# Holding an adaLN result back until the blocks of h are out, in a one-core decoder trunk

## The chip, the cores and the metric

One core of one Trainium2 chip runs the whole program in one launch. The metric is the device time of an execution in microseconds (us), here the median of several. A profile is one execution recorded by the hardware. PE is TensorE (PEld its weight loads), ACT is ScalarE, DVE is VectorE, POOL is GpSimd and SP is SyncE, which here issues the loads of the weights.

## The reference, cut to what matters

There are two layers of three sub-layers each, so six in a row, for 288 tokens (256 of a prompt, 32 of eight short sequences). Each sub-layer normalizes x, scales and shifts it (adaLN), runs its own mixing, normalizes the result, gates it and adds it to x.

```
def _pre(x, c, g_pre, ada_w, ada_b):
    mod = jax.nn.silu(c) @ ada_w + ada_b
    shift, scale, gate = jnp.split(mod[:, None, :], 3, axis=-1)
    return _rms_norm(x, g_pre) * (1 + scale) + shift, gate

def _post(x, y, gate, g_post, res_w):
    return x + res_w * (1 + gate) * _rms_norm(y, g_post)
```

Sub-layers 0, 2, 3 and 5 are SwiGLU feed-forwards, sub-layer 1 is windowed attention beside a gated linear recurrence (the even mixer), and sub-layer 4 is HGRN2 (the odd mixer). The adaLN product `silu(c) @ ada_w` depends on c alone, so it can be worked out at any time before its sub-layer needs it.

## The kernel before

Activations lie with features on the 128 partitions, in eight blocks of 128 features by 288 tokens. Every fp32 product is made of three: weights and activations are split into a high and a low part (`whi`, `wlo` from `raw`; `h` in two halves), and PE adds high by high, high by low and low by high in one PSUM tile. `pj` is an input projection, `y` an output projection.

The order of PE's and SP's instructions is that in which the program writes them. The other engines' instructions are put in order by the framework's scheduler, except where the program ties them into chains. To choose the order of PE's work the program keeps a clock of its own while it writes (`clk["t"]`), with a guess of how long each instruction takes. Where this clock says that PE would wait (`until`), the program inserts a piece of adaLN product as a filler (`ada_next`, `ada_half`) or a warming product (`warm`). Work with several stages is a generator in a list of `sides`; `run_sides` resumes each one when the program's clock has reached the time at which its inputs should be ready.

The adaLN product of a sub-layer comes in twelve chunks, eight for shift and scale and four for the gate, each a 1 MB load `aw` by SP and four matmuls `ada` (or eight on half the columns). A full set ends in `ada_finish`: ACT copies the PSUM tile `ada` to `asb`, PE transposes and folds it (`adaT`), and DVE makes `mod` and `modA` or `modG` from it.

Between two sub-layers (a crossing; there are five) everything depends on the tokens' sums. `out_proj` works out the two inverse roots, PE spreads them over the partitions (`yivb`, `xivb`), and `pre` makes the eight blocks of h: DVE updates x and makes `hv`, POOL scales the samples' part, ACT writes the high part of `h`, DVE the low part. ACT, DVE and POOL do this in chains `da`, `dv` and `dg`; on ACT an activation table (`tab`) follows. Then `proj_in` begins with a group of four output tiles over the eight blocks, 96 products `pj` in all, block by block as h comes. `x_stats`, a side with ACT squares (`xsq`), POOL adds and PE sums (`xms`), starts about then too. In the even mixer POOL also issues its loads and the copies of old cache rows, and it fills the edges of the convolution's input (`xr<-cin`) and takes its new state out (`rgo<-xr`).

Of the kernel before, what the change touches and what calls it, by code (L numbers as in the profile page):

```python
# [49 lines left out]
def tile_trunk(ctx: ExitStack, tc: tile.TileContext, I: dict, O: dict):  # L50
    nc = tc.nc
    SY = nc.sync
    clk = {"t": 0.0, "dma": 0.0, "step": 0.0}
# [86 lines left out]
    def flat(name, dt=F32):  # L140
        return bp.tile([128, 2 * PW], dt, tag="b", name=name)

    def dbl(name, dt=F32, w=NT):
        return flat(name, dt).rearrange("p (c t) -> p c t", c=2)[:, :, :w]

    def tmp(name, w=NT):
        return tp.tile([128, PW], F32, tag="t", name=name)[:, :w]

    def small(name, shape, tag=None, bufs=None):
        return sp.tile(shape, F32, tag=tag or "s%d" % int(np.prod(shape[1:])), name=name, bufs=bufs)  # L150

    def aux_ps(name):
        return ps.tile([128, 512], F32, tag="ps", name=name, bufs=8)
# [59 lines left out]
    def act(out, in_, f, **kw):  # L213
        r = A.activation(out, in_, f, **kw)
        if last_table[0] is not None:
            tc.add_manual_dep(r.ins, last_table[0], NOSYNC, reason="activation table order")
        last_table[0] = r.ins.name
        return r
# [32 lines left out]
    def side(gen, *aps):  # L251
        sides.append([max(clk["t"], ready(*aps)), gen])
# [180 lines left out]
    def mod_of(i):  # L433
        if i not in mods:
            mods[i] = (mp.tile([128, 24, 9], F32, tag="mod", name=f"mod{i}", bufs=3),
                       mp.tile([128, 8, 9], F32, tag="modA", name=f"modA{i}", bufs=3),
                       mp.tile([128, 8, 9], F32, tag="modG", name=f"modG{i}", bufs=3))
        return mods[i]
# [9 lines left out]

    def ada_finish(i, g, acc):
        mod, mA, mG = mod_of(i)  # L450
        asb = flat("asb")[:, :512]
        A.activation(asb, acc, AF.Copy)
        yield [asb]
        pt = aux_ps("adaT")
        o, nj = (16, 2) if g else (0, 4)
        for b in range(4):
            if g:
                T.matmul(pt[:, 18 * b:18 * b + 18], lhsT=asb[:, 128 * b:128 * b + 128], rhs=foldg, start=True, stop=True)
            else:
                T.transpose(pt[:, 128 * b:128 * (b + 1)], asb[:, 128 * b:128 * (b + 1)], ident)  # L460
        m = 9 if g else 32
        V.tensor_tensor(
            out=mod[:, o:o + 4 * nj, :].rearrange("p (j b) m -> p b j m", b=4),
            in0=pt[:, :4 * nj * m].rearrange("p (b j m) -> p b j m", b=4, j=nj)[:, :, :, 0:9],
            in1=adab[:, 24 * i + o:24 * i + o + 4 * nj].rearrange("p (j b) -> p b j", b=4).unsqueeze(3)
            .to_broadcast([128, 4, nj, 9]),
            op=OP.add)
        V.scalar_tensor_tensor(out=mG if g else mA, in0=mod[:, 8 + 8 * g:16 + 8 * g, :], scalar=1.0,
                               in1=(gph if g else gpre)[:, 8 * i:8 * i + 8].unsqueeze(2).to_broadcast([128, 8, 9]),
                               op0=OP.add, op1=OP.mult)  # L470
# [20 lines left out]
    def ada_steps(parts):  # L491
        n = ada_st["n"]
        ada_st["n"] += 1
        i, c = chunks[n]
        ada_load_to(n)
        g = int(c >= NC0)
        if c in (0, NC0):
            ada_st["acc"] = aux_ps(f"ada{i}{g}")
        acc = ada_st["acc"]
        w = aw[n][0]  # L500
        m = 512 // parts
        for q in range(parts):
            if q:
                yield
            for j in range(4):
                k = 2 * (c - NC0) + j // 2 if g else c
                T.matmul(acc[32 * j:32 * j + 32, m * q:m * q + m], lhsT=sc[:, k, :],
                         rhs=w[:, 512 * j + m * q:512 * j + m * q + m],
                         start=c in (0, NC0) and q == 0, stop=c in (NC0 - 1, NCH - 1) and q == parts - 1)
        ada_load_to(n + AW)  # L510
        if c in (NC0 - 1, NCH - 1):
            side(ada_finish(i, g, acc))
# [21 lines left out]
    def table(f):  # L534
        return act(small("tab", [128, 1]), eps, f)
# [40 lines left out]
    def spread(u, name, gap):  # L576
        until(u, gap=gap, step=ada_half)
        p = aux_ps(name)[:, :NT]
        for j in range(4):
            T.matmul(p[:, NG * j:NG * j + NG], lhsT=pick[:, j, :], rhs=u, start=True, stop=True)  # L580
        return p

    def x_stats(prior=None):
        w = small("xw", [128, NG], tag="xw", bufs=2)
        clk["xw"] = w
        if prior:
            yield 12.0
        t0 = flat("xsq")[:, :2 * NT]
        for b in range(0, NB, 2):
            t = flat("xsq")[:, :2 * NT] if b else t0  # L590
            r = A.activation(t, x[:, b:b + 2, :].rearrange("p c t -> p (c t)"), AF.Square)
            if prior:
                after(r, prior)
            if b:
                (G if prior else V).tensor_tensor(out=t0, in0=t0, in1=t, op=OP.add)
        yield
        p = aux_ps("xms")[:, :NG]
        for c in range(2):
            sums(p, t0[:, NT * c:NT * c + NT], c == 0, c == 1)
        V.tensor_scalar(out=w, in0=p, scalar1=EPS, scalar2=None, op0=OP.add)  # L600

    def h_tiles():
        hp = [mp.tile([128, 2, 2, NT], F32R, tag=f"h{u}", name=f"h{u}", bufs=1) for u in range(NB // 2)]
        for t in hp:
            parts[t.tensor.name] = {}
        return hp, [hp[b // 2][:, b % 2] for b in range(NB)]
# [3 lines left out]
    def h_mark(b, lo):  # L610
        h_times[b, lo] = clk["end"]
# [36 lines left out]
    def pre(i, iv, ivx, ys, v, a, g):  # L648
        mod, mA, _ = mods[i]
        hp, hk = h_tiles()  # L650
        vt = {}

        def view(b, n, t):
            return t[:, b:b + n, :] if n > 1 else t[:, b, :]

        def wide(p, n):
            return p.unsqueeze(1).to_broadcast([128, n, NT]) if n > 1 else p

        def update(b, n):
            y, xb = ys(b, n), view(b, n, x)  # L660
            v.tensor_tensor(out=y, in0=y, in1=wide(iv, n), op=OP.mult)
            v.tensor_tensor(out=xb, in0=xb, in1=y, op=OP.add)

        def scale(b, n):
            t = dbl(f"hv{b}") if n > 1 else tmp(f"hv{b}").unsqueeze(1)
            for q in range(n):
                vt[b + q] = (t, q)
            v.tensor_tensor(out=t if n > 1 else t[:, 0, :], in0=view(b, n, x), in1=wide(ivx, n), op=OP.mult)
            ts = t[:, :, NPR:].rearrange("p b (s t) -> p b s t", t=TS)
            for m, op in ((mA, OP.mult), (mod, OP.add)):  # L670
                g.tensor_tensor(out=ts, in0=ts, in1=m[:, b:b + n, 1:9].unsqueeze(3).to_broadcast([128, n, NSQ, TS]), op=op)
            for q in range(n):
                c = b + q
                p = t[:, q, :NPR]
                a.activation(hk[c][:, 0, :NPR], p, AF.Identity, scale=mA[:, c, 0:1], bias=mod[:, c, 0:1])
                if q == 0:
                    a.activation(hp[b // 2][:, b % 2:b % 2 + n, 0, NPR:], t[:, :, NPR:], AF.Copy)
                h_mark(c, 0)
                a.activation(p, p, AF.Identity, scale=mA[:, c, 0:1], bias=mod[:, c, 0:1])

        def low(b, n):
            h = hp[b // 2][:, b % 2:b % 2 + n]
            v.tensor_tensor(out=h[:, :, 1, :], in0=vt[b][0], in1=h[:, :, 0, :].bitcast(F32), op=OP.subtract)
            for q in range(n):
                h_mark(b + q, 1)

        update(0, 1)
        scale(0, 1)
        update(1, 1)
        scale(1, 1)  # L690
        low(0, 1)
        update(2, 2)
        scale(2, 2)
        low(1, 1)
        update(4, 2)
        scale(4, 2)
        low(2, 2)
        update(6, 2)
        scale(6, 2)
        low(4, 2)  # L700
        low(6, 2)
        return hk
# [88 lines left out]
    def out_proj(i, nk, hk):  # L791
# [105 lines left out]
        iv = spread(u, "yivb", GAPS[2])  # L897
        ivx = spread(ux, "xivb", GAPS[3])
        hk = pre(i + 1, iv, ivx, ys, dv, da, dg)
        da.add(table(AF.Sigmoid if i % 3 == 0 else AF.Silu))  # L900
        clk["prior"] = (da.last, dv.last)
        if i < NSUB - 2:
            side(x_stats(da.last))
        return hk
# [727 lines left out]
```

## Time and profile before

| what | value |
|---|---|
| median of 3 runs | 1341.95 us (1340.23 to 1341.97) |
| the profiled execution's own time | 1341.75 us |
| its span, first to last instruction | 1340.0 us |
| what lies around the span | 1.75 us |
| PE busy | 1277.4 us, 95% of the span |
| TensorE's mean granted clock | 0.981 of full |

PE is nearly always busy, so the time is close to PE's work and its gaps. The crossings' spreads `xivb` start at 262.7, 421.6, 656.9, 884.7 and 1108.5 us; the even mixer lies between the first two. PE's fp32 matmuls are recorded twice each, so `adaT x8` is four instructions.

### The profile page before, as it was taken

To read this page: it belongs to the slowest core of one execution; us is meant where nothing else is said; L and a number is where in the kernel's file an instruction comes from. 1 tells how busy PE (TensorE), PEld (TensorE's weight loads), DVE (VectorE), ACT (ScalarE), POOL (GpSimd) and SP (SyncE) were. 2 spreads that over 40 slices of the span, in tenths; PEclk is the share of its full clock that TensorE was granted. 3 is DMA by queue.
4 is the path that set the end of the run, shared out by engine and by line. 5 is a ranking of instruction groups with operands and counts; after the bars stand their busy time and mean duration, and the time that the engine had idled before them with its cause. 6 is when DMAs were issued, how large, how long until landed. Compare 5 with 4: busy or idle time off the path is not lost.

```text
span 1340.0 us, 25184 instructions
## 1 busy us (share of the span) xinstructions
PE 1277.4 (95%) x10381; PEld 1182.8 (88%) x10381; DVE 781.6 (58%) x1411; ACT 636.9 (48%) x1087; POOL 198.3 (15%) x298
## 2 busy tenths in 40 slices
PE   9999999969887999999999999999999998999996
PEld 8999999857666899999889999987878988999995
DVE  6634545538738355555655555558888877555432
ACT  5434444446645454444454444454534566444441
POOL 0000002054013100002110000225333231000011
PEclk9999999979989999999999999999999999999998
DMA  8777465477545754454566455467444352555441
GB/s 360 270 299 262 179 224 212 153 261 266 211 191 189 281 190 158 162 180 162 192 259 242 158 167 179 159 227 305 171 162 159 134 182 71 189 170 176 158 158 36
DMA packets 39555, 263.46 MB, mean 197 GB/s; under 512 B 4932, under 2 KB 5764, under 8 KB 9360
## 3 DMA queue, kind: packets, MB, share of 16 engines
q1 hardware_dynamic: 35280, 249.09, 50.9%
q0 software_dynamic: 4160, 12.77, 2.8%
q8 instruction: 81, 1.33, 0.4%
q14 instruction: 34, 0.28, 0.1%
HBM read 254.69 MB, written 7.15 MB: 195 GB/s over the span
## 4 chain that ended last, share of the span: by engine, by line
PE 83%; DVE 7%; ACT 4%; issue 2%; DMA 1%; POOL 1%; SPq 0%; DVEq 0%; POOLq 0%; ACTq 0%
PE pj L94 48%; PE y L94 24%; PE ada L94 3%; DVE wlo L94 1%; PE lv L94 1%; POOL hv L94 1%; PE adaT L94 1%; ACT hv L94 1%; DVE x L94 1%; ACT whi L94 1%; DVE hv L94 1%; ACT L94 1%; PE o L94 1%; DVE yg L94 1%; ACT h L94 1%
## 5 line engine op out<-in xcount | busy, mean ns | idle before, releaser
L94 PE MATMUL pj<-h,whi 128*128 128x288 f32 x3552 | 724.4, 299 | 2.0 <-ACT h L94 1.8
L94 PEld LDWEIGHTS pj<-h,whi 128*128 128x128 f32 x3552 | 571.0, 189 | 31.4 <-issue 19.6
L94 DVE TENSOR_TENSOR wlo<-raw,whi 128x1024 fp32r<-128x1024 f32 x326 | 399.9, 1237 | 301.6 <-ACT whi L94 301.1
L94 ACT ACTIVATE whi<-raw 128x1024 fp32r<-128x1024 f32 x326 | 340.6, 1057 | 381.8 <-PE pj L94 154.0
L94 PE MATMUL pj<-h,wlo 128*128 128x288 f32 x1776 | 519.1, 295 | 0.9 <-DVE wlo L94 0.9
L94 PEld LDWEIGHTS pj<-h,wlo 128*128 128x128 f32 x1776 | 336.1, 189 | 1.5 <-DVE wlo L94 1.4
L94 PE MATMUL y<-mh,whi 128*128 128x288 f32 x1408 | 281.3, 295 | 0.0
L94 PEld LDWEIGHTS y<-mh,whi 128*128 128x128 f32 x1408 | 226.0, 188 | 2.1 <-issue 1.7
L94 PE MATMUL y<-mh,wlo 128*128 128x288 f32 x704 | 208.0, 295 | 0.0
L94 POOL TENSOR_TENSOR yss<-yss,ysq 128x288 f32<-128x288 f32 x55 | 59.3, 1079 | 812.6 <-ACT ysq L94 804.9
L94 PEld LDWEIGHTS y<-mh,wlo 128*128 128x128 f32 x704 | 132.5, 188 | 0.0
L94 DVE TENSOR_TENSOR fs<-fs,pj 128x288 f32<-128x288 f32 x88 | 39.5, 452 | 94.8 <-PE pj L94 93.1
L94 PE MATMUL ada<-aw,cT 128*32 128x256 f32 (+1 forms) x696 | 68.9, 500 | 1.5 <-DMA aw<-in_w_ada 1.5
L94 ACT ACTIVATE mh<-fs 128x288 fp32r<-128x288 f32 x88 | 37.7, 433 | 56.1 <-DVE fs L94 56.1
L94 ACT ACTIVATE fs<-pj 128x288 f32<-128x288 f32 x88 | 34.7, 399 | 38.9 <-PE pj L94 38.9
L94 DVE TENSOR_TENSOR mh<-fs,mh 128x288 fp32r<-128x288 f32 x88 | 39.5, 452 | 10.2 <-ACT mh L94 10.2
L94 PE MATMUL y<-o,whi 128*128 128x288 f32 x192 | 39.1, 297 | 0.5 <-DVE o L94 0.5
L94 ACT ACTIVATE ysq<-y 128x288 f32<-128x288 f32 x42 | 17.0, 404 | 47.4 <-PE y L94 47.4
L94 ACT ACT_TABLE_LOAD x27 | 34.6, 1283 | 7.6 <-DVE oivw L94 5.4
L94 PEld LDWEIGHTS ada<-aw,cT 128*32 128x32 f32 x696 | 17.3, 111 | 21.6 <-issue 15.2
L94 ACT ACTIVATE h<-hv,mod,modA 128x256 fp32r<-128x256 f32 x40 | 23.7, 592 | 21.0 <-DVE hv L94 21.0
L94 DVE TENSOR_TENSOR yg<-y,modG 128x32 f32<-128x32 f32 x48 | 8.9, 186 | 40.6 <-ACT yg L94 40.6
(287 smaller groups left out, 1090.4 us busy)
## 6 DMA issues: line engine op xcount, KB each, us to landing
raw<-in_wf_in SPq DMA_DIRECT2D x88, 1024.0 KB, 4.9
aw<-in_w_ada SPq DMA_DIRECT2D x64, 1024.0 KB, 6.5
raw<-in_wf_out SPq DMA_DIRECT2D x44, 1024.0 KB, 4.9
raw<-in_wo_in SPq DMA_DIRECT2D x16, 1024.0 KB, 7.2
awf<-in_w_ada SPq DMA_DIRECT2D x8, 1024.0 KB, 9.3
raw<-in_we_in SPq DMA_DIRECT2D x7, 1024.0 KB, 7.1
raw<-in_we_out SPq DMA_DIRECT2D x4, 1024.0 KB, 8.1
S<-in_s POOLq DMA_DIRECT2D x16, 256.0 KB, 5.9
```

The source lines that it names most:

```text
L94: r = f(*args, **kw)
```

## The change

At the end of `pre` the program notes when, by its own clock, the last block of h is done (`clk["busy"]`, taken before the table is loaded) and keeps it as `clk["hold"]`. An `ada_finish` that is resumed before that time yields until it, and only then has ACT copy the result. One that is resumed before `pre` was written sees the hold of an earlier crossing, which has passed, and is not held.

```
     def ada_finish(i, g, acc):
         mod, mA, mG = mod_of(i)
+        if clk["t"] < clk.get("hold", 0.0):
+            yield clk["hold"] - clk["t"] + 0.01
         asb = flat("asb")[:, :512]
         A.activation(asb, acc, AF.Copy)
         yield [asb]
...
         hk = pre(i + 1, iv, ivx, ys, dv, da, dg)
+        clk["busy"] = clk["end"]
         da.add(table(AF.Sigmoid if i % 3 == 0 else AF.Silu))
         clk["prior"] = (da.last, dv.last)
+        clk["hold"] = clk["busy"]
```

The numbers of products `pj` and `y`, of warming products and of chunks stay as they were (some chunks are cut in halves that were whole, and the other way), but because the program's clock runs on differently, fillers and sides move in the whole program behind the first crossing. On PE at the first crossing (`adaT` folds the gate of sub-layer 1, `ada` is a chunk of a later one), this piece of the difference stands just behind the first eight `pj`:

```order
 L94 MATMUL pj_2998<-h_2894,whi 128x288
 L94 MATMUL pj_2998<-h_2894,wlo 128x288
-L94 MATMUL adaT<-sm,asb 128x18 x4
+L94 MATMUL ada_3024<-aw_0_2877,cT 32x256 x4
 L94 MATMUL pj_2995<-h_2894,whi 128x288
```

The fold has left this place and half a chunk has taken it. In the changed kernel the fold stands behind the group of 96, ahead of the next output tile (`pj_3180`):

```order
L94 MATMUL ada_3024<-aw_2_3014,cT 32x512 x4
L94 MATMUL adaT<-sm,asb 128x18 x4
L94 MATMUL pj_3180<-h_2894,whi 128x288 x2
L94 MATMUL pj_3180<-h_2894,wlo 128x288
L94 MATMUL pj_3180<-h_2894,whi 128x288 x2
L94 MATMUL pj_3180<-h_2894,wlo 128x288
L94 MATMUL xms<-xsq,mean_88 32x72 x8
```

So all of the group now comes ahead of the fold. ACT's copy `asb` still follows the table, and now three squares `xsq`, one `whi` and the fourth square stand between. At the second crossing the fold (of the next shift and scale) moves in the same way, to just behind `xms`; at the third a gate's fold, which stood some twenty `pj` behind the second crossing's group, now comes ahead of the first `pj`; and at the fourth one leaves that place for the end of the group. The fifth is unchanged.

On POOL, behind the first crossing's blocks of h and the even mixer's transfers, the adds of x's squares and the copies around `xr` change places:

```order
 L94 TENSOR_TENSOR xsq<-xsq 128x576
 L94 MEMSET xr_2985 128x3
 L94 COPY xr_2985<-cin 128x8x3
+L94 COPY rgo<-xr_2985 128x3
+L94 COPY rgo<-xr_2985 128x24
 L94 MEMSET xr_2985 128x3
 L94 COPY xr_2985<-cin 128x8x3
+L94 COPY rgo<-xr_2985 128x3
+L94 COPY rgo<-xr_2985 128x24
 L94 MEMSET xr_2986 128x3
 L94 COPY xr_2986<-cin 128x8x3
+L94 TENSOR_TENSOR xsq<-xsq 128x576
```

The second add now stands behind four copies out of `xr`, and the third behind two more; before, all eight copies followed the last add.

On ACT at the end of the even mixer (`sms` are the samples' scores, `gx` the gelu branch, `m` its product, `pTs` transposed scores, which PE waits for), before:

```order
L94 ACTIVATE sms,den<-sms,mx 128x288
L94 ACTIVATE es<-es 128x1
L94 ACT_TABLE_LOAD
L94 ACTIVATE gx_2993<-gx_2993 128x2x288
L94 ACTIVATE gx_2994<-gx_2994 128x2x288
L94 ACT_TABLE_LOAD
L94 ACTIVATE tab<-eps 128x1
L94 ACTIVATE m_3919<-ob 128x288
L94 ACTIVATE m_3925<-ob 128x288
L94 ACTIVATE m_3931<-ob 128x288
L94 ACTIVATE m_3937<-ob 128x288
L94 ACTIVATE pTs<-pT 128x512
```

and in the changed kernel:

```order
L94 ACTIVATE sms,den<-sms,mx 128x288
L94 ACTIVATE es<-es 128x1
L94 ACT_TABLE_LOAD
L94 ACTIVATE gx_2993<-gx_2993 128x2x288
L94 ACTIVATE o_3902<-pv_3539 128x128
L94 ACTIVATE pTs<-pT 128x512
```

Two copies `pTs` stood behind all of this before; now one does, behind one table load and half of the gelu.

## Rows read from the trace of the kernel before

**Rows 1.** The page, busy us (share of the span) and instructions of PE and others.

```profile
PE 1277.4 (95%) x10381; PEld 1182.8 (88%) x10381; DVE 781.6 (58%) x1411; ACT 636.9 (48%) x1087; POOL 198.3 (15%) x298
```

**Rows 2.** What PE waited for: us in total, times, longest us.

```profile
PE adaT L94 <- ACT asb L94: 23.3, 4, 13.5
PE pv L94 <- ACT pTs L94: 8.3, 1, 8.3
PE lv L94 <- DVE Q L94: 3.1, 4, 2.4
PE rgr L94 <- DVE xc L94: 2.7, 1, 2.7
...
PE ada L94 <- DMA aw<-in_w_ada: 1.5, 1, 1.5
```

**Rows 3.** Stretches: us, busy us (instructions), then granted clock, DMA share, GB/s.

```profile
262.70:297.90 35.20, 21.57 (x165) 18.48 (x161) 13.59 (x23) 15.27 (x31) 16.09 (x33) 0.76 0.81 292
...
268.60:285.60 17.00, 5.12 (x24) 4.81 (x28) 7.69 (x13) 11.46 (x22) 10.99 (x19) 0.50 0.67 227
...
367.60:381.10 13.50, 9.21 (x32) 3.63 (x36) 4.16 (x15) 5.80 (x13) 0.00 (x0) 0.50 0.17 50
429.00:439.20 10.20, 5.25 (x32) 4.24 (x32) 6.17 (x10) 9.05 (x18) 2.00 (x4) 0.50 0.21 90
...
656.90:676.30 19.40, 17.88 (x156) 15.46 (x152) 11.93 (x20) 13.76 (x28) 5.54 (x11) 1.00 0.88 347
...
666.10:676.20 10.10, 10.10 (x76) 10.02 (x76) 4.33 (x6) 8.61 (x17) 3.12 (x5) 1.00 0.82 317
```

**Rows 4.** Timeline of the first crossing: start, us, instruction, [idle before <- released by].

```profile
262.70 1.11 PE L94 MATMUL xivb<-xiv,pick 128*128 128x72 f32 x8
...
266.66 0.29 PE L94 MATMUL pj<-h,wlo 128*128 128x288 f32 x1
...
278.51 0.76 DVE L94 TENSOR_TENSOR h<-hv,h 128x576 fp32r<-128x576 f32 x1 [3.01 <-ACT hv L94]
...
279.85 0.58 ACT L94 ACTIVATE asb<-ada 128x512 f32<-128x512 f32 x1
...
280.32 2.39 ACT L94 ACTIVATE xsq<-x 128x576 f32<-128x576 f32 x4
...
280.48 1.89 PE L94 MATMUL adaT<-sm,asb 128*128 128x18 f32 x8 [13.52 <-ACT asb L94]
```

**Rows 5.** Timeline of PE in the third crossing.

```profile
662.66 0.64 PE L94 MATMUL ada<-aw,cT 128*32 128x256 f32 x8 [1.49 <-DMA aw<-in_w_ada]
...
681.65 0.66 PE L94 MATMUL adaT<-ident,asb 128*128 128x128 f32 x4 [0.65 <-ACT asb L94]
```

**Rows 6.** Timeline of POOL behind the first crossing.

```profile
283.91 0.55 POOL L1028 DMA_DIRECT2D out_v_old<-vc  x1 [0.18 <-issue]
284.48 1.42 POOL L94 TENSOR_TENSOR xsq<-xsq 128x576 f32<-128x576 f32 x1
...
286.56 2.93 POOL L94 TENSOR_TENSOR xsq<-xsq 128x576 f32<-128x576 f32 x2
298.05 2.37 POOL L94 COPY rgo<-xr 128x3 f32<-128x3 f32 x8 [8.56 <-ACT xr L94]
```

**Rows 7.** Timeline of PE and ACT at the end of the even mixer.

```profile
361.97 1.06 PE L94 MATMUL ada<-aw,cT 128*32 128x512 f32 x8
...
365.96 1.28 ACT L94 ACT_TABLE_LOAD   x1
367.25 1.26 ACT L94 ACTIVATE gx<-gx 128x576 f32<-128x576 f32 x2
...
369.93 1.43 ACT L94 ACTIVATE m<-ob 128x288 fp32r<-128x288 f32 x4
...
371.89 1.97 PE L94 MATMUL pv<-pTs,vt 128*64 128x512 f32 x2 [8.27 <-ACT pTs L94]
```

**Rows 8.** Timeline of PE in the second crossing.

```profile
433.94 1.11 PE L94 MATMUL adaT<-ident,asb 128*128 128x128 f32 x4 [7.59 <-ACT asb L94]
```

More of the change, by code (lines that the diff above doesn't have):

```diff
@@ L450, in ada_finish @@
         mod, mA, mG = mod_of(i)
+        if clk["t"] < clk.get("hold", 0.0):
+            yield clk["hold"] - clk["t"] + 0.01
         asb = flat("asb")[:, :512]
@@ L899, in out_proj @@
         hk = pre(i + 1, iv, ivx, ys, dv, da, dg)
+        clk["busy"] = clk["end"]
         da.add(table(AF.Sigmoid if i % 3 == 0 else AF.Silu))
         clk["prior"] = (da.last, dv.last)
+        clk["hold"] = clk["busy"]
         if i < NSUB - 2:
```

## Prediction, on record before the run

> **What bounds the kernel now.** I read the page first: PE is busy for 1277.4 of 1340.0 us, no other engine for over 58% [rows 1]. The work on PE is the same in both kernels (as many products `pj` and `y`, as many chunks of adaLN, as many warming products), so the time moves only with PE's gaps and with its clock. The waits of PE come next: the longest by far is that of the fold `adaT` for ACT's copy `asb`, 23.3 us in four waits, and then one wait of `pv` for `pTs`, 8.3 us [rows 2]. The clock by stretches shows what such a wait costs beyond itself: behind the last `pj` ahead of the first fold, at 267.0 (266.66 and 0.29, [rows 4]), TensorE's clock goes to its lower level, 1.2 of 2.4 GHz, and stays there from 268.6 to 285.6; two more such stretches lie around the long wait for `pTs` and the fold of the second crossing [rows 3]. The reader should see in the timeline why the first fold waits 13.52 us: PE takes its instructions in order, ACT writes all of h first, so `asb` starts at 279.85, and the 88 products left of the group of 96 stand behind the fold although their blocks of h come one by one in that time [rows 4].
>
> The third crossing has no fold at that place. From its spread to the end of the 96 products it takes 19.4 us, against 35.2 in the first [rows 3], with one wait of 1.49 us for a chunk's load [rows 5]. This is my model of a crossing after the change.
>
> **First crossing.** The change takes the fold out of the group. Gone: 13.5 us of waiting. Gone too is the half clock: PE was busy for 5.12 us in that stretch [rows 3], which at full clock is half, so 2.6. New: the filler that takes the fold's place needs its load; I take 1.5 us as in [rows 5]. The blocks of h don't forbid this: the last low part ends at 279.27 (278.51 and 0.76, [rows 4]), and eight products at 0.133 (10.10 us for 76, [rows 3]) follow, so the group could end at 280.3; the model says 262.7 + 19.4 + 0.5 for half a chunk more = 282.6. The fold then waits for `asb`, which stands behind four squares (2.39 us, [rows 4]) and a split; in the third crossing the fold behind the squares waited 0.65 [rows 5]; I take 0.7. Sum: -13.5 - 2.6 + 1.5 + 0.7 = -13.9 us.
>
> **Behind it, a new wait.** PE comes to `xms` at 282.6 + 1.0 (a chunk, [rows 7]) + 0.7 + 1.0 (the fold, half of 1.89 at half clock, [rows 4]) + six products 0.8 = 286.1. Before, `xms` came after the three adds of POOL had long ended at 289.5 (286.56 and 2.93, [rows 6]). Nothing moves the first add forward: it stands behind the transfers, at 284.48, until 285.9. Then come 0.7 us of edges (from there to 286.56), two adds of 2.93 together and six copies out of `xr` at 0.3 (2.37 for 8), [rows 6], and each pair of these waits for ACT's `xr`, some 0.3 each by estimate: 285.9 + 0.7 + 2.9 + 1.8 + 0.9 = 292.2. PE waits 6.1 us. If the copies held up nothing the adds would end at 289.5 as now and the wait would be 3.4; if the transfers or `xr` come later by one add, 7.6. I take 6.1, since the order puts the copies ahead. A wait of 6.1 lies between one of 2.7 [rows 2] behind which no half-clock stretch lies and 7.6 [rows 8] with one; I charge 2.6 for the clock, and nothing as the other bound. In return, by 292 the convolution has had its input for long, so the wait of `rgr` for `xc`, 2.7 [rows 2], goes. Sum: +6.1 + 2.6 - 2.7 = +6.0 us.
>
> **End of the even mixer.** PE now waits 8.3 for `pTs`, 0.6 later on, and loses half of 9.21 us to the clock, 4.6 [rows 3, 7]: 13.5. In the new order ACT has one table load and half of the gelu ahead of the awaited `pTs` and not two loads, the gelu and four `m`: 1.28 + 0.63 + 0.3 for one `o` (an estimate) = 2.2 in place of 5.4 (365.96 to the end of `m`, 371.36) [rows 7], 3.2 less. PE has two more `pv` in front of it (1.0 each, half of 1.97 at half clock, [rows 7]), a transpose and nine `pj` (0.6 and 1.2 at the pace above), 3.8 us, of which ACT's copies for them take back 2.0 by estimate. That leaves a wait of 8.3 - 3.2 - 3.8 + 2.0 = 3.3. The last copies `pTss` now stand behind the second load, 1.3, and 0.5 is for the fold moved to the end: 5.1 in all, and I leave the clock up. Bounds: 0 and 13.5, since the chain from scores to `pTs` may have its own length. I take -8.4 us.
>
> **The other crossings.** Second: -7.6 [rows 8] - 2.6 (half of 5.25, [rows 3]) + 1.5 + 0.7 (both as in [rows 5]) = -8.0. Third: the fold behind `xms` goes, -0.65; the gate's fold that comes in takes 1.0 of PE, which lies in the 1.49 us that PE waits there for a load [rows 5]: -0.7. Fourth: its fold leaves such a place, so 0.5 of that load's wait is new, and `asb` behind the squares costs 0.7: +1.2. The fifth is unchanged. In the odd mixer the order of sides shifts. PE's waits there, `lv` 3.1 [rows 2] and some others, may go either way; I take 0 and keep 4 us either way for the range.
>
> **Sum.** -13.9 + 6.0 - 8.4 - 8.0 - 0.7 + 1.2 = -23.8. Against the profiled execution's own 1341.75 (1340.0 of span and 1.75 around it) this is 1317.95; the median of the runs is 0.2 above it, so 1318.
>
> **A rule weighed.** In the three half-clock stretches, 17.0, 13.5 and 10.2 us long, I count half of PE's busy time, 5.12, 9.21 and 5.25, as lost, 9.8 in all [rows 3], because the rest was waiting whatever the clock. The Trainium skill, in "TensorE: Matmul & The Clock Gate", section Terms, takes the whole throttled time: the penalty is about that time times the share of the clock withheld. By it the stretches would cost 20.3 (half of 40.7, an estimate by that page), and the change would give up to 10.5 more.
>
> **Rivals.** (1) The waits only move: `xms` waits as said and the mixer's end keeps its 13.5 us. For it: the softmax chains there run on DVE and ACT and PE is moved, not they. Against: the awaited copy really has 3.2 us less ahead of it. Then -15.4 us and 1326; with waits of 4 us more in the odd mixer 1330. (2) The wait at `xms` doesn't come, because ACT and POOL are through earlier: 8.7 less, 1309. Against it stands the order on POOL. (3) The clock costs half of the whole stretch and not of the busy time: 10.5 more, 1307.5. It would need a delay of the waiting engines too. Against it: only the products in a stretch can be slow, and they are recorded. (It is the rule above of the Trainium skill, "TensorE: Matmul & The Clock Gate", section Terms.) (4) Slower: the odd mixer. There POOL's transfers `out_s_s` of one tree now stand ahead of a later level's product for `K`, and a transfer waits for DVE's new state; POOL stands still meanwhile, `K` is late and PE's `lv` waits. The price is one wait per tree, four trees: at 8 us each 32, so 1350; it decides from 23.8 / 4 = 6 us each, where the longest wait of `lv` is now 2.4 [rows 2]. (5) Nothing changes: each gap is filled by waits for h or loads. The third crossing's 19.4 us speak against it: 1342.
>
> **How the numbers follow.** Chances: my forecast, 1312 to 1325, 0.62; (1) 0.19; (2) 0.10; (3) 0.04; (4) 0.03; (5) 0.02. About 0.2% is what a measurement of this kernel can tell from no change. Faster: 0.62 + 0.19 + 0.10 + 0.04 = 0.95, same 0.02, slower 0.03. The range runs from 1308, case (2) and a quiet end of the mixer, to 1330, case (1) with the odd mixer's 4 us; it leaves out (3) to (5) and the edges of the others.
>
> **What would show it.** In the changed profile the first crossing should take about 20 us from spread to the end of the group, at full clock throughout; the waits of `adaT` should fall from 23.3 to about 3 in total; a wait of `xms` for POOL's `xsq` of some 6 us should be new, with a half-clock stretch behind it; the wait for `pTs` should be under 5 us. I am wrong if the group of 96 still stops for blocks of h or loads for over 5 us, if `xms` finds its sums ready, if the mixer's end takes as long as before, or if the odd mixer grows.

## The result, and the profile after

The median of four runs is 1326.03 us (1322.38 to 1329.77) against 1341.96 for the kernel before; the ratio is 0.9874, with a 95% interval of 0.9852 to 0.9896. A second set of six runs of the same kernel, told of below, gave 1324.23 and 0.9853 (0.9828 to 0.9879). The change makes the kernel faster by 16 to 20 us. 1318 was predicted, with a range of 1308 to 1330; 1326.03 lies just above the forecast's own 1312 to 1325, and 1324.23 just inside.

The profiled execution took 1327.57 us, with a span of 1325.5. Of the page, the line on PE, which answers to [rows 1]:

```profile
PE 1282.6 (97%) x10397; PEld 1185.8 (89%) x10397; DVE 779.3 (59%) x1411; ACT 635.9 (48%) x1087; POOL 196.7 (15%) x298
```

What PE waited for (total us, times, longest), which answers to [rows 2]:

```profile
PE xms L94 <- POOL xsq L94: 8.8, 1, 8.8
PE pv L94 <- ACT pTs L94: 2.8, 1, 2.8
PE xyms L94 <- DVE ysq L94: 2.4, 1, 2.4
PE ada L94 <- DMA aw<-in_w_ada: 2.4, 2, 1.4
...
PE krt L94 <- ACT kr L94: 2.3, 1, 2.3
...
PE adaT L94 <- ACT asb L94: 0.7, 1, 0.7
```

The waits of the fold `adaT` went from 23.3 us to 0.7, and the one for `pTs` from 8.3 to 2.8. In their place stands one wait of 8.8, of the sums `xms` for POOL. Two more are new. One of 2.4, of `xyms`, lies at the end of the even mixer's output projection, where DVE makes two low parts of weights (2.35 us together) ahead of the awaited `ysq`; one of 2.3, of `krt`, lies in the odd mixer.

Stretches of the changed kernel (us; busy us and instructions of PE, PEld, DVE, ACT and POOL; granted clock; DMA share; GB/s), which answer to [rows 3]: the first crossing, the half-clock stretch behind it, the products from `xms` to `rgr`, then the even mixer's end from the first `pvs` to `xyms` and the half-clock stretch in it.

```profile
264.90:285.00 20.10, 18.59 (x166) 15.69 (x165) 12.04 (x21) 13.96 (x28) 9.29 (x19) 1.00 0.93 360
291.20:301.40 10.20, 4.67 (x33) 2.83 (x33) 8.35 (x11) 2.00 (x2) 6.01 (x19) 0.50 0.84 311
296.70:305.70 9.00, 8.97 (x63) 5.95 (x64) 8.52 (x17) 2.31 (x3) 0.51 (x2) 0.74 0.67 247
367.90:402.80 34.90, 34.90 (x261) 32.25 (x265) 18.99 (x32) 17.31 (x37) 11.51 (x10) 0.85 0.54 203
369.70:379.90 10.20, 10.20 (x53) 8.07 (x52) 1.07 (x6) 1.92 (x7) 0.00 (x0) 0.50 0.95 363
```

The first crossing takes 20.1 us at the full clock, where it took 35.2 with half of it at the lower clock. The wait behind it and the mixer's end have half-clock stretches of their own, though, and in the second of these PE was busy all the time.

PE's timeline (start, us, instruction, idle before and what ended it) at the first crossing's fold, the end of the even mixer and the second crossing's fold, which answers to [rows 4, 7, 8]:

```profile
285.97 1.07 PE L94 MATMUL adaT<-sm,asb 128*128 128x18 f32 x8
...
362.23 1.40 PE L94 MATMUL pv<-pTs,vt 128*64 128x512 f32 x2 [2.77 <-ACT pTs L94]
...
367.89 0.43 PE L94 MATMUL pvs<-pTss,vt 32*64 32x128 f32 x2 [0.62 <-ACT pTss L94]
...
437.50 0.66 PE L94 MATMUL adaT<-ident,asb 128*128 128x128 f32 x4 [0.66 <-ACT asb L94]
```

(Transposes are recorded once each, so `adaT<-ident x4` is four instructions, here and in [rows 5, 8].)

How long each part of the program took, from one spread `xivb` to the next (us, from the starts of the spreads in each profile; the experiments follow below):

| kernel | to crossing 1 | 1 to 2 | 2 to 3 | 3 to 4 | 4 to 5 | 5 to the end |
|---|---|---|---|---|---|---|
| before | 262.7 | 158.9 | 235.4 | 227.7 | 223.8 | 231.5 |
| changed | 264.9 | 147.9 | 227.4 | 229.4 | 223.3 | 232.5 |
| changed, second profile | 262.8 | 142.2 | 227.4 | 229.5 | 227.3 | 232.5 |
| e1_fold_back_4 | 263.7 | 146.6 | 227.4 | 229.4 | 235.3 | 234.8 |
| e2_second_only | 263.4 | 158.8 | 228.9 | 230.9 | 239.4 | 232.2 |
| e5_copies_late | 262.8 | 146.6 | 227.4 | 229.4 | 225.3 | 231.3 |
| e7_loads_first | 262.9 | 140.4 | 227.6 | 229.3 | 223.7 | 233.1 |
| e3_transfers_late | 263.2 | 139.8 | 227.4 | 229.5 | 224.0 | 232.4 |
| e8_warm | 262.9 | 137.1 | 227.6 | 229.5 | 222.6 | 232.6 |
| e9_gates_later | 263.3 | 151.2 | 229.7 | 228.9 | 226.5 | 232.6 |

The change moves chunks of adaLN too: 19.5, 8.5, 9 and 12 lie in the four middle columns before, 16, 9, 11 and 13 after. At 1.0 us a chunk this is -3.5, +0.5, +2.0 and +1.0 us of work that is only moved. Without it the four columns changed by -7.5, -8.5, -0.3 and -1.5 in the first profile of the changed kernel, and by -13.2, -8.5, -0.2 and +2.5 in the second.

### The profile page after: what moved, and what is told of

Same layout as the page of the kernel before. It is cut to its first block, busy times and chain, and to the rows that moved or that the text cites. A ratio compares the mean times of both kernels' runs of the same rounds, so it can differ in the third digit from the quotient of the medians.

```text
span 1325.5 us, 25215 instructions
## 1 busy us (share of the span) xinstructions
PE 1282.6 (97%) x10397; PEld 1185.8 (89%) x10397; DVE 779.3 (59%) x1411; ACT 635.9 (48%) x1087; POOL 196.7 (15%) x298
## 4 chain that ended last, share of the span: by engine, by line
PE 83%; DVE 7%; ACT 5%; POOL 2%; issue 1%; DMA 1%; DVEq 0%; SPq 0%; ACTq 0%; POOLq 0%
PE pj L94 47%; PE y L94 24%; PE ada L94 3%; DVE wlo L94 2%; PE lv L94 1%; POOL hv L94 1%; ACT hv L94 1%; PE o L94 1%; DVE x L94 1%; PE warm L94 1%; ACT L94 1%; ACT whi L94 1%; DVE yg L94 1%; DVE hv L94 1%; PE adaf L94 1%
## 5 line engine op out<-in xcount | busy, mean ns | idle before, releaser
L94 PE MATMUL ada<-aw,cT 128*32 128x256 f32 (+1 forms) x712 | 72.1, 505 | 2.4 <-DMA aw<-in_w_ada 2.4
L94 PEld LDWEIGHTS ada<-aw,cT 128*32 128x32 f32 x712 | 17.6, 112 | 21.3 <-issue 15.2
```

What stands on the lines that cost most here:

```text
L94: r = f(*args, **kw)
```

## The experiments

PE's order is the changed kernel's throughout in e3_transfers_late, e5_copies_late and e7_loads_first, and up to the fourth crossing in e1_fold_back_4. In e8_warm it differs at the place named, in e9_gates_later from the first `rgr` on, and in e2_second_only it is that of the kernel before up to the second crossing. Each diff is against the changed kernel where nothing else is said.

**Is the price of a fold in the group the same elsewhere?** The hold is set at the first crossing only. Up to the fourth crossing PE's order stays what it was. So at the second crossing the hold does nothing: the fold went from there because the program's clock runs on differently behind the first.

```
-        clk["hold"] = clk["busy"]
+        clk["hold"] = clk["busy"] if i == 0 else 0.0
```

> The hold is set at the first crossing only. PE's instructions are then the changed kernel's up to the fourth crossing; there the gate's fold `adaT` stands behind the first eight `pj` of the group of 96 again, as it did at the first crossing before the change. Theory (a fold in the group costs the wait for `asb` and the half clock): the fold waits 12 to 14 us there, the fourth crossing's spread-to-group time goes from about 20 to 33 to 35 us, and the time to 1326 + 13.9 = about 1340 us. Rival (the place costs little where ACT has less to do than at the first crossing): the wait is under 5 us and the time 1326 to 1330 us.

Measured: 1335.49 us, ratio 0.9945 (0.9915 to 0.9976). PE's timeline at the fourth crossing, and the half-clock stretch around it:

```profile
879.55 1.90 PE L94 MATMUL adaT<-sm,asb 128*128 128x18 f32 x8 [8.15 <-ACT asb L94]
```

```profile
873.90:884.00 10.10, 4.45 (x19) 4.45 (x20) 6.76 (x11) 8.65 (x19) 2.92 (x6) 0.50 0.27 99
```

The fold waits 8.15 us, and the stretch from crossing 4 to 5 is 12.0 us longer than in the changed kernel's first profile, 8.0 longer than in its second. The theory holds in kind, with a smaller price than expected: 8 us of waiting here where 12 to 14 were said, and 13.5 at the first crossing [rows 4]. So of the first four crossings the hold works at two, the first and the fourth. I had not counted the fourth, since in the kernel before its fold happened to lie ahead of the first `pj`.

**Are the crossings' gains separate terms?** The hold is set at the second crossing only; up to there PE's order is that of the kernel before.

```
-        clk["hold"] = clk["busy"]
+        clk["hold"] = clk["busy"] if i == 1 else 0.0
```

> The hold is set at the second crossing only. PE's instructions are the earlier kernel's up to the second crossing, so the first crossing keeps its fold's wait of 13.5 us and the mixer its wait of 8.3 us. Theory (the crossings' gains are separate terms): the second crossing's wait of 7.6 us goes, and the time is 1342 - 8 = 1334 us, with up to 3 us either way from the moved order behind it. Rival (the gains hang together, since the later fillers have moved): 1340 or more.

Measured: 1354.86 us, ratio 1.0089 (1.0055 to 1.0123), slower than before. PE's timeline at the fourth crossing:

```profile
894.36 1.89 PE L94 MATMUL adaT<-sm,asb 128*128 128x18 f32 x8 [8.19 <-ACT asb L94]
```

At the second crossing the fold's wait of 7.6 us went, as expected, and its part went from 235.4 to 228.9 us. But 2.0 of that is two moved chunks, so 4.5 us are left where 8 were expected: `xms` and the fold wait 0.9 and 0.8 us there now, and a half-clock stretch of 3.4 us stands behind them. And behind it the program's clock runs on differently: a fold falls into the group at the fourth crossing, where no hold guards it now, and waits 8.19 us; from crossing 4 to 5 it takes 15.6 us more than before, one chunk of it. My theory failed in its "up to 3 us either way". A change to this program's clock is worth what it moves everywhere behind it. The two runs speak for a hold at every crossing, since the place of a fold there hangs on all that the clock did ahead of it; the fourth is the only one, beside the first, at which this was seen.

**What makes POOL late?** The timeline of POOL behind the first crossing, first the transfers of the kernel before (the fourth is the first line of [rows 6]), then the changed kernel:

```profile
280.19 0.76 POOL L1027 DMA_DIRECT2D out_k_old<-kc  x1 [0.53 <-issue]
281.30 0.56 POOL L1028 DMA_DIRECT2D out_v_old<-vc  x1 [0.35 <-DMA vc<-in_vc]
282.96 0.77 POOL L1027 DMA_DIRECT2D out_k_old<-kc  x1 [1.10 <-DMA kc<-in_kc]
```

```profile
284.15 0.76 POOL L1031 DMA_DIRECT2D out_k_old<-kc  x1 [2.25 <-DMA kc<-in_kc]
286.11 0.56 POOL L1032 DMA_DIRECT2D out_v_old<-vc  x1 [1.19 <-DMA vc<-in_vc]
288.23 0.77 POOL L1031 DMA_DIRECT2D out_k_old<-kc  x1 [1.56 <-DMA kc<-in_kc]
290.27 0.55 POOL L1032 DMA_DIRECT2D out_v_old<-vc  x1 [1.27 <-DMA vc<-in_vc]
290.84 1.41 POOL L94 TENSOR_TENSOR xsq<-xsq 128x576 f32<-128x576 f32 x1
...
295.29 1.39 POOL L94 TENSOR_TENSOR xsq<-xsq 128x576 f32<-128x576 f32 x1
```

The first add starts 25.9 us behind the spread (290.84 - 264.94), where it started 21.8 behind it before (284.48 - 262.70). The four transfers ahead of it wait 6.3 us for their own loads (2.25 + 1.19 + 1.56 + 1.27), where these waits were 1.4 for the loads and 0.7 for issue. Three more profiles with the same loads and transfers have 7.1 (the second profile), 6.7 (e5_copies_late) and 8.7 us (e1_fold_back_4), and PE's wait of `xms` is 9.6, 8.4 and 11.2 us in them. From its start to the end of the third add it is 5.84 us (to 296.68), and 5.01 before (284.48 to 289.49): the copies cost 0.8. Two experiments take this apart. In the first the transfers, and with them the copies, go behind the adds:

```
-        for c in range(2):
-            G.dma_start(O["k_old"][:, 4 * c:4 * c + 4, :], kcv[c][:, :, TS:])
-            G.dma_start(O["v_old"][:, 4 * c:4 * c + 4, :], vcv[c][TS:])
+        def old(prior):
+            for c in range(2):
+                after(G.dma_start(O["k_old"][:, 4 * c:4 * c + 4, :], kcv[c][:, :, TS:]), prior)
+                after(G.dma_start(O["v_old"][:, 4 * c:4 * c + 4, :], vcv[c][TS:]), prior)
...
-                G.tensor_copy(rgo[:, 12 + 24 * j:36 + 24 * j].rearrange(...), groups(t, X0)[:, :, 4:7])
+                r = G.tensor_copy(rgo[:, 12 + 24 * j:36 + 24 * j].rearrange(...), groups(t, X0)[:, :, 4:7])
+                if j == 3:
+                    old(r)
```

> PE's order is that of the changed kernel. On POOL the four transfers of old cache rows and the copies out of `xr` stand behind the three adds of `xsq`. Theory A (PE's new wait of 8.8 us for `xsq` is the transfers' wait for their loads, 6.3 us in four pieces, ahead of the first add): the wait falls under 2 us and the half-clock stretch behind it goes, 8.8 - 1 + 2.3 = some 10 us less: 1316 us, or 1319 if the wait of `rgr` for `xc` comes back with its 2.7. Theory B (the copies hold the adds, as in the prediction, 2.7 us): the wait falls to about 6 and the time to 1323 us. Rival C (whatever PE does not wait for here it waits for a few us later, for `xc` or for `kr`): 1324 us or more, with a wait as long elsewhere.

Measured: 1318.21 us, ratio 0.9807 (0.9778 to 0.9835). Its POOL timeline, and its PE waits:

```profile
281.71 2.95 POOL L94 TENSOR_TENSOR xsq<-xsq 128x576 f32<-128x576 f32 x2 [1.53 <-ACT xsq L94]
...
286.49 1.42 POOL L94 TENSOR_TENSOR xsq<-xsq 128x576 f32<-128x576 f32 x1
...
291.30 0.78 POOL L1033 DMA_DIRECT2D out_k_old<-kc  x1
```

```profile
PE rgr L94 <- DVE xc L94: 4.0, 2, 3.6
PE pv L94 <- ACT pTs L94: 2.8, 1, 2.8
```

The adds now wait for ACT's squares only, and PE's wait for them is gone. As expected, `rgr` waits for `xc` again, 4.0 us, with a half-clock stretch of 3.4 us behind it. Theory A holds, and the time is near the 1319 that it gave for this case. (The scheduler also moved a few instructions of ACT and DVE; PE's and SP's order is the same.) In the second experiment the transfers stay and only the copies go behind the adds:

```
-                G.tensor_copy(rgo[:, 3 * j:3 * j + 3], t[:, NPR:NPR + 3])
+                after(G.tensor_copy(rgo[:, 3 * j:3 * j + 3], t[:, NPR:NPR + 3]), clk["xsq"])
```

(the same for the second copy; `clk["xsq"]` is the last add).

> PE's order is that of the changed kernel, and the four transfers keep their place; only the copies `rgo` out of `xr` stand behind the last add of `xsq`. Theory A (the transfers hold POOL): the wait of `xms` falls from 8.8 by no more than 1 us, and the time stays within 1 us of the changed kernel's 1326. Theory B (the copies hold it): it falls by 2.7 us to about 6, and the time to 1323 us.

Measured: 1324.85 us, ratio 0.9859 (0.9836 to 0.9881), the changed kernel's within both intervals. Its timelines of PE and POOL:

```profile
289.12 1.41 POOL L94 TENSOR_TENSOR xsq<-xsq 128x576 f32<-128x576 f32 x1
...
291.20 2.86 POOL L94 TENSOR_TENSOR xsq<-xsq 128x576 f32<-128x576 f32 x2
```

```profile
294.11 0.35 PE L94 MATMUL xms<-xsq,mean 128*32 128x72 f32 x4 [8.35 <-POOL xsq L94]
```

The adds take 4.94 us from the first to the last and not 5.84. The wait is 8.35 us, against 8.8 to 11.2 with the copies in their place; it did not fall to 6. The copies were worth under 1 us; the transfers carried the rest.

**Why do the transfers' loads come late?** One experiment issues the loads of `kc` and `vc` ahead of three others in the program. On POOL they pass two of them, `cs` and `msk`; `rot` goes out long before.

```
+        for c in range(2):
+            load(kch[c][:, :512], I["kc"][:, 512 * c:512 * (c + 1)])
+            load(vch[c][:, :512], I["vc"][:, 512 * c:512 * (c + 1)])
         load(rot, I["rot"])
         cs = dbl("cs")
...
-        for c in range(2):
-            load(kch[c][:, :512], I["kc"][:, 512 * c:512 * (c + 1)])
-            load(vch[c][:, :512], I["vc"][:, 512 * c:512 * (c + 1)])
```

> The changed kernel with POOL's loads `kc` and `vc` ahead of those of `rot`, `cs` and `msk`; PE's order is the same, and the transfers and copies keep their places. Theory A (the first add of `xsq` is late by the transfers' wait for these loads): they are issued some 3 us sooner, the four waits fall from 6.3 us to about 3, the wait of `xms` from 8.8 to about 5.5, and the time by 4 us, half clock and all, to 1322. Rival (the loads land when the queue of SP's 1 MB loads lets them, whenever they are issued): the waits stay at 6 us and the time at 1326.

Measured: 1319.13 us, ratio 0.9817 (0.9793 to 0.9840), against 0.9853 (0.9828 to 0.9879) for the unaltered changed kernel on the same chip. POOL's timeline in it:

```profile
280.50 0.76 POOL L1031 DMA_DIRECT2D out_k_old<-kc  x1 [0.97 <-DMA kc<-in_kc]
282.34 0.56 POOL L1032 DMA_DIRECT2D out_v_old<-vc  x1 [1.08 <-DMA vc<-in_vc]
284.53 0.78 POOL L1031 DMA_DIRECT2D out_k_old<-kc  x1 [1.63 <-DMA kc<-in_kc]
287.07 0.55 POOL L1032 DMA_DIRECT2D out_v_old<-vc  x1 [1.76 <-DMA vc<-in_vc]
287.64 1.41 POOL L94 TENSOR_TENSOR xsq<-xsq 128x576 f32<-128x576 f32 x1
```

How long the two loads `kc` took from issue to landing (KB each, median us), first in the kernel before, then in the changed kernel, then here (`vc`: 4.8, 8.1 and 9.4):

```profile
kc<-in_kc POOLq DMA_DIRECT2D x2, 256.0 KB, 4.1
```

```profile
kc<-in_kc POOLq DMA_DIRECT2D x2, 256.0 KB, 6.5
```

```profile
kc<-in_kc POOLq DMA_DIRECT2D x2, 256.0 KB, 7.9
```

SP's loads in the same crossing, first in the kernel before, then in the changed kernel:

```profile
261.97 24.95 SPq L429 DMA_DIRECT2D aw<-in_w_ada  x4
287.01 0.38 SPq L317 DMA_DIRECT2D raw<-in_we_in  x1
```

```profile
264.20 9.77 SPq L429 DMA_DIRECT2D aw<-in_w_ada  x4
274.07 0.38 SPq L317 DMA_DIRECT2D raw<-in_we_in  x1
```

In the changed kernel SP's first 1 MB load `raw` goes out 9.1 us behind the spread (274.07), and 24.3 before (287.01), because the four loads `aw` ahead of it are out in 9.8 us and not 25.0. From 11.3 to 21.3 us behind the spread the DMA engines are busy for 0.97 of the time, against 0.72 before. The Trainium skill, in "Trainium Kernel Development and Optimization", section Key Constraints, says that transfers issued from SP, ACT and POOL run on the same 16 DMA engines and interleave. The landing times of `kc` agree with it, 4.1 us at 0.72 and 6.5 at 0.97; among the profiles of the new order they don't follow the share (7.0 at 0.99 in the second profile, 7.9 at 0.98 here, 9.5 at 0.89 in e1_fold_back_4). No run took SP's loads away, so that it is they is argued from these numbers, not shown.

What issuing the loads sooner is worth stays open. The four waits add up to 5.4 us here, neither 3 nor 6, and `xms` waits 7.9 us. The loads went out 1.6 to 3.8 us sooner, counted from the spread, and the first add starts 24.8 us behind the spread, 1.1 and 1.9 us sooner than in the changed kernel's two profiles. That is less than theory A asked for. But SP's `raw` went out sooner too in this execution, 7.8 us behind the spread and not 9.1 as in those two. In e1_fold_back_4 it went out after 7.8 us as well, with POOL's loads in their old place, and against that profile the first add is 3.6 us sooner, as theory A has it. One profile of each can't part the two. The times don't settle it either: their two intervals overlap, and of the 4.5 us of span between this profile and the changed kernel's second one 3.6 lie between crossings 4 and 5, where the two programs are the same.

**How steady are the half-clock stretches?** The changed kernel was profiled once more.

> The changed kernel once more, unaltered, for a second profile. Theory (where the short half-clock stretches fall differs from one execution to the next, and each takes about half of PE's busy time in it): the waits are the same to 1 us (`xms` 8 to 9, `pTs` 2.8, `ysq` 2.4), the time is 1322 to 1330 us, and where a stretch of products stands at another clock than in the first profile its length differs by half the time at the lower clock. Rival (the clock's stretches belong to the order of the work): they stand at the same places with the same lengths, and the time is within 1 us of the first profile's.

Measured: 1324.23 us, ratio 0.9853 (0.9828 to 0.9879). The wait behind the first crossing, and two stretches that hold the instructions from `xms` to `rgr` and from the first `pvs` to `xyms`, as in the rows of the first profile above:

```profile
295.34 0.71 PE L94 MATMUL xms<-xsq,mean 128*32 128x72 f32 x16 [9.59 <-POOL xsq L94]
```

```profile
295.30:303.60 8.30, 8.26 (x63) 5.92 (x64) 7.81 (x16) 2.31 (x3) 0.52 (x2) 0.80 0.61 231
365.80:396.00 30.20, 30.20 (x257) 28.58 (x257) 18.91 (x32) 17.19 (x37) 11.52 (x10) 1.00 0.62 240
```

The waits are the same to 0.8 us, and the mixer's end takes 30.2 us at the full clock where the first profile had 34.9 with 10.2 of it at the lower clock. Between the profiles the program did not differ; the clock did. The rival falls at the mixer's end; behind the first crossing the stretch is 10.2 us long in both.

**What brings the clock down at the mixer's end?** To e3_transfers_late eight warming products are added ahead of the last `pv` (three transposes `pTs` move with it, from behind two chunks of adaLN to ahead of them):

```
+                if kv and not n:
+                    warm(8)
                 pv4 = pts.rearrange("p (h c q) -> p h c q", h=hg, c=n + 1)
```

> As e3_transfers_late, with eight warming products (0.29 us each, 2.3 us) ahead of the last product `pv` in the even mixer, whose wait for `pTs` is 2.8 us there. Theory (idle time of PE at the mixer's end is what brings the clock down): no half-clock stretch stands between the awaited `pv` and the output projection, and the time is that of e3_transfers_late, 1318, or up to 3 us under it; the wait shrinks to about 0.5. Rival 1 (the warming products are simply work, since `pTs` is ready when they end or earlier): up to 2 us slower than e3_transfers_late. Rival 2 (the clock falls there for another cause): a stretch of 3 us or more stays there.

Measured: 1314.16 us, ratio 0.9779 (0.9755 to 0.9802). PE's timeline there, and the stretch that holds this wait and the `pvs`:

```profile
352.64 2.05 PE L94 MATMUL warm<-ones 128*128 128x128 f32 x16
355.47 1.07 PE L94 MATMUL pv<-pTs,vt 128*64 128x512 f32 x2 [0.78 <-ACT pTs L94]
```

```profile
354.70:364.80 10.10, 8.53 (x76) 4.56 (x76) 4.87 (x18) 6.97 (x21) 0.00 (x0) 1.00 0.77 287
```

The warming products end 0.78 us ahead of `pTs`, so they take nothing from PE (from the transpose ahead of them to the awaited `pv` it is 4.4 us with and without them), and no half-clock stretch lies between here and the output projection. In each of the six profiles with this order and without the warming products one of 3.4 us lies at this place, and in three of them (the changed kernel's first, e1_fold_back_4 and e5_copies_late) a second one some 3 to 7 us behind it. The theory fits; as one profile shows the absence, it is not more than that. From the awaited `pv` to the first `pvs`, waits aside, the same products take 3.4 us, and 4.85 in e3_transfers_late. From crossing 1 to 2 it takes 137.1 us, 2.7 less than in e3_transfers_late, but that is not the warming products' doing: 2.7 us are gained ahead of them, where the two programs are the same, 1.3 at their place, and 1.25 are lost behind it, where a half-clock stretch follows the wait of `xyms` here and none there. This is the best version of the study: its interval lies below that of the changed kernel on the same chip (0.9828 to 0.9879) and well below the kernel before. Against e3_transfers_late alone, whose interval reaches from 0.9778 to 0.9835, the gain of the warming products is not settled by the times.

**Can the next wait be moved on as well?** In e3_transfers_late, `rgr` waits 4.0 us for `xc`; here the convolutions begin later by the program's clock.

```
-CV = (0.5, 1.5)
+CV = (7.0, 1.5)
```

> As e3_transfers_late, with the convolutions of the even mixer begun 6.5 us later by the program's clock, so that the first two products `rgr` stand some twenty `pj` further back. Theory (the wait of 4.0 us for `xc` in e3_transfers_late is a place chosen too early): it falls under 1 us, and the time goes to about 1314 us. Rival (each shift of the program's clock moves later folds and fillers, as with the hold at the second crossing alone): the wait goes, but waits of about as much stand elsewhere, at the mixer's end or at later crossings, and the time is 1318 us or more.

Measured: 1326.83 us, ratio 0.9864 (0.9833 to 0.9894). PE's waits between the first and the second crossing:

```profile
PE pv L94 <- ACT pTs L94: 5.6, 2, 5.0
PE pT L94 <- DVE sm L94: 3.2, 2, 2.6
PE rp L94 <- ACT rx L94: 2.2, 2, 1.2
```

The rival is right: the wait for `xc` is gone, and 11.0 us stand at the attention's chains, against 2.8 for `pTs` and 0.9 for `pT` in e3_transfers_late. With them goes the clock: from 359.9 to 387.2 the granted clock is 0.56. The profile is of the slowest of the five executions (1334.05 us), so how much of the median's 8.6 us over e3_transfers_late lies there is not shown.

## Why the prediction came out as it did

The direction and the range held, and rival (1)'s 1326 is what was measured, but not by its mechanism, so that agreement is luck: the mixer's end did get shorter in its waits. The predicted sum was -23.8 us; the profiles have -14.2 and, in the second, some -18.4 of span. From the first crossing to the second I had -16.3 (-13.9 + 6.0 - 8.4), and -7.5 and -13.2 were measured; so nearly all of the miss in the first profile, and over half of it in the second, lies there, behind the first crossing's fold. Step by step:

**First crossing, -13.9.** Right. Up to the end of the group and the fold it took 35.2 us, and 20.6 now with the chunk and a half (1.5 us) that came in taken off: -14.6. The fold ends 22.1 us behind the spread (285.97 + 1.07 - 264.94); my steps gave 285.3 - 262.7 = 22.6. It waits for nothing, where I had 0.7.

**The new wait of `xms`, +6.0.** The wait was foreseen, with PE's arrival right to half a microsecond (23.0 us behind the spread; 23.4 said), and its size was not: 8.8 and 9.6 us in the two profiles, 11.2 in e1_fold_back_4, beyond my upper bound of 7.6. The step that failed is "Nothing moves the first add forward: it stands behind the transfers, at 284.48". Nothing moves it forward, but something moves it back, by 4.1 us: the transfers' waits for their loads, which went from 1.4 to 6.3 us (e3_transfers_late takes the transfers away, and the wait with them). I held the transfers' time fixed, although they wait for loads; that these land late because a faster PE has SP's loads asked for sooner is argued above, not shown. The copies that I charged with 2.7 us cost 0.8 (e5_copies_late). The clock behind the wait cost 2.1 us where I charged 2.6, and the wait of `rgr`, 2.7, went as said.

**End of the even mixer, -8.4.** The waits came out near: 2.77 for `pTs` (3.3 said), 0.62 for `pTss` (1.3 said), nothing for the moved fold (0.5 said) and 0.8 for `pT`, which I had not counted: 4.2 together where I had 5.1. What failed is "I leave the clock up". In the first profile two stretches at the half clock lie there, of 3.4 and 10.2 us. The same instructions at the full clock (the second profile) show the price of the longer: 34.9 - 30.2 = 4.7, some 0.45 for each us, and so 1.5 for the shorter; e8_warm, without the shorter, shows 1.45. In the second profile only the shorter one was there. Before, the waits were 8.3 + 0.6 and the clock 0.45 x 9.21 = 4.1, 13.0 in all; now it is 4.2 + 6.2 = 10.4 in one execution and 4.2 + 1.5 = 5.7 in the other. The term was -2.6 or -7.3, and a single number for it was too sure.

**Not foreseen.** The wait of `krt`, 2.3; the wait of `xyms`, 2.4 in place of 0.8, and 1.2 for a short half-clock stretch behind it in the first profile. Parts of the program whose instructions did not change differ too: 2.2 us up to the first crossing in the first profile, 1.0 behind the fifth.

**Crossings 2, 3, 4: -8.0, -0.7, +1.2.** Measured, without the moved chunks: -8.5, -0.3, and -1.5 or +2.5 in the two profiles, the last with the odd mixer in it. The second is right in size, though it is not the hold that moves the fold there (e1_fold_back_4). Between crossings 4 and 5 the second profile has a half-clock stretch of 6.8 us, at 930, that the first lacks. Rival (4), the odd mixer, fell: the waits of `lv` there are 0.2 us in all, and 1.0 in the second profile.

**The rule weighed.** The two half-clock stretches of 10.2 us tell the two readings apart. In the one where PE was busy for 4.67 us, the products from `xms` to `rgr` took 8.92 us against 6.85 in e3_transfers_late, which ran them at the full clock: 2.1 us lost. In the other, where PE was busy throughout, 4.6 to 4.7 were lost. Half of the busy time would be 2.3 and 5.1. The Trainium skill's rule in "TensorE: Matmul & The Clock Gate", section Terms, gives 5.1 for each: it comes near the second and is far above the first, and here the measurement decides for the busy time, at some 0.45 us for each. From `xms` to `rgr` in e8_warm, where PE was busy through a stretch of 3.4 us, it is 8.40 us, 1.55 lost: 0.45 again.

## What to carry to other kernels

When a wait of the bound engine goes, the loads behind it are asked for sooner, as SP's were here by 15 us: look for the engine that waits for a landing in its own queue, such as POOL with transfers here, and put the work that the bound engine needs ahead of it. Where a program's own clock sets the order, a local edit is an edit of everything behind it; read the whole order again, and guard each place where a long wait is possible and not only the one that shows it now. Price the lower clock by PE's busy time in it, and give a term that hangs on it both ends.

## What was not expected of the hardware

Identical instructions ran at different clocks from one execution to the next. In the list from the first `pvs` to `xyms`, 10.2 us were at the half clock in one profile of the changed kernel and in e5_copies_late, 3.4 in e1_fold_back_4, none in the second profile, in e3_transfers_late, e7_loads_first and e8_warm; it took 34.9, 34.9, 31.8 and four times 30.3 us. The four runs of the changed kernel spread over 7.4 us, in step with their mean granted clock (1322.4 us at 0.986, 1329.8 at 0.979). Also, the same loads `kc` of 256 KB, issued at the same place, took 6.5, 7.0, 6.8 and 9.5 us (median) to land in four profiles (the changed kernel's two, e5_copies_late and e1_fold_back_4).
